# Summing the modulation columns with transposes and a free-axis reduction, in place of one-column matmuls

## The chip, the cores and the metric

The kernel runs on one core of one Trainium2 chip. The metric is the device time of one execution in microseconds, the median of a few runs. The engines of the core are named as in the profile: PE is TensorE (PEld its weight loads), DVE is VectorE, ACT is ScalarE, POOL is GpSimd and SP is SyncE, which here only issues DMAs. Each engine takes its instructions in the order in which they were written into its own queue and stops at the first one whose inputs are not there.

## The reference, cut to what matters

Two blocks follow each other on 256 tokens of width 2048. The first has two layers; each is steered by a modulation of two conditioning vectors, `c` (for the tokens) and `c_ctx` (for 256 context tokens):

```
def _layer(x, ctx, c, c_ctx, ...):
    shift, scale, gate = split(silu(c) @ w_mod + b_mod, 3)      # 2048 -> 3 * 2048
    hx = rmsnorm(x, norm_w) * (1 + scale) + shift
    a_h, a_b, a_c, a_z, q, k, v, r_z = split_in(hx @ w_in)
    mod_c = silu(c_ctx) @ w_mod + b_mod                         # layer 1: shift and scale alone
    hc = rmsnorm(ctx, norm_w) * (1 + mod_c[d:2*d]) + mod_c[:d]
    ...                                                         # retention and convolution branches
    x = x + gate * (concat(y_conv, y_ret) @ w_out)
    ctx = ctx + mod_c[2*d:] * (concat(yc_conv, yc_ret) @ w_out) # layer 0 alone
```

The second block (attention, a feed-forward part, a gated projection) uses no modulation.

## The kernel before, in words

All large products run on PE as split products: a weight tile of 256 rows by 512 columns is loaded in fp32 (tile `raw`, pool `wraw` with four buffers, issued by SP), split into a high part by ACT (`whi`, L277) and a low part by DVE (`wlo`, L278), and multiplied in three passes (L332). `Block.run` goes over the 16 k-tiles of a weight two at a time; two k-tiles are a unit, so a block of 512 columns has 8 units. PE's order is written by hand: it is the order of the calls in the program. The other engines' instructions are put in order by a scheduler that goes by priorities; the split has a raised one, as have the statistics of a norm (`hot()`).

Small work is woven between the units. `pump()` (L264) is called after every unit and lets each queue in `pumps` take a step. A queue is a `Side` object (L226): it holds generators, and a step runs one of them to its next `yield`. The queue `modq` holds `mod_bg` and steps at a rate: two steps in three units in layer 0 (`Side(1, 1, 2, 3)`, L898), one in three in layer 1 (L918). `drain()` (L251) runs what is left at once.

`mod_bg` (L422) computes the modulation on DVE, one block of 512 columns at a time. For each of eight pairs of k-tiles it loads 256 rows by 512 columns of `w_mod` (L429) and adds each row, times the partition's value of silu(c) or silu(c_ctx), to an accumulator [128, 512] (`macc0` for the first vector, `macc1` for the second, one buffer each): L435 for the first row block, L438 for the other 15. That is one step, and there are eight of them. The accumulator then still has to be summed over its 128 partitions, and the sums have to stand with features on partitions, 128 to a column. This is what L441 to L447 do: four matmuls for each vector with the accumulator as weights and a column of ones as the moving operand, and `mod_add` (L449, L450), which adds the bias.

The first call of `mod_bg`, queued before layer 0, has 12 column blocks with two vectors: the gates of layer 0 and the shift and scale of layer 1. What is not done at the end of layer 0 is drained there (L904). The second call has 4 column blocks with one vector, the gates of layer 1.

What surrounds the end of layer 0: the last block of `w_out` (L850), its result added to the streams `xr` and `cr_` (tags `a` and `b`) on DVE (L856), their squares on ACT (L871) and the sums of squares on DVE (L872, tiles `sqa`); then `modq.drain()`; then the modulation columns times the norm weight (L907); then `pli_proj` (L877), a product that depends on neither block and that stands there to occupy PE, with the norm's sums (L209), rsqrt on POOL (L195) and broadcast (L219, L220) between its pieces; then layer 1, whose operands (`make_hx`, L497) need the norm and all shift and scale columns of layer 1.

PSUM is split into five main tiles (`mm`) and three side tiles (`sd`, `side_ps`), the latter shared by retention, norms, transposes and the modulation sums.

Of the kernel before, what the change touches and what calls it, by code (L numbers as in the profile page):

```python
# [30 lines left out]

# columns of the constant tables
CA = {}
# [17 lines left out]

# rows of the packed feature vectors
VEC_ROWS = [
# [60 lines left out]
def kernel(ctx: ExitStack, tc: tile.TileContext, x, c, cx, c_ctx, norm_w, w_mod, b_mod,  # L114
# [31 lines left out]

    # ------------------------------------------------------------------ small tables
    ca = mk(consts, [P, NCA], "ca")
# [38 lines left out]

    # ------------------------------------------------------------------ helpers
    def hot():
# [14 lines left out]
    def tok_sums(accs):  # L204
        """per-token sums over the features of [128 feature, 256 token] tiles, tokens on partitions"""
        ps = side_ps()
        for a, acc in enumerate(accs):
            for t in range(2):
                nc.tensor.matmul(ps[:, 2 * a + t:2 * a + t + 1], lhsT=acc[:, t * P:(t + 1) * P],  # L209
                                 rhs=ones[:, 0:1], start=True, stop=True)  # L210
        return ps[:, :2 * len(accs)]

    def bcast_rows(r, n, tag):
        """[128 token, n] columns to a [128, n*128] tile with the value of each token on all partitions"""
        ps = side_ps()
        for t in range(n):
            dg = mk(sm, [P, P], "dg")
            with hot():
                nc.vector.tensor_scalar(out=dg, in0=ident, scalar1=r[:, t:t + 1], scalar2=None, op0=ALU.mult)  # L219
            nc.tensor.matmul(ps[:, t * P:(t + 1) * P], lhsT=ones, rhs=dg, start=True, stop=True)  # L220
        o = mk(sm, [P, n * P], tag, bufs=1)
        with hot():
            nc.scalar.copy(out=o, in_=ps[:, :n * P])
        return o

    class Side:  # L226
        """side work in steps, woven between the units of the products: at most `act` items under way,
        `rate` steps per unit, num units in den"""

# [27 lines left out]
    def pair(pool, n, tag):  # L257
        """room for the hi and lo parts of n columns"""
        b = mk(pool, [P, 2, n], tag, F32R)
        return b[:, 0, :], b[:, 1, :], b  # L260
# [20 lines left out]
    class Block:  # L281
        """columns cols = [(first, width)] of a weight against the moving operands mov(k) -> (hi, lo).
        fm: features on partitions, a [128, T] tile per 128 columns; tm: tokens on partitions, a
        [128, width] tile per column group and 128 tokens"""

        def __init__(self, w, cols, mov, T, mode, nk, dst=None):
            self.w, self.cols, self.mov, self.T, self.mode, self.nk = w, cols, mov, T, mode, nk
            self.done = 0
            self.dst = dst or self.room
            self.nt = [wd // P if mode == "fm" else T // P for _, wd in cols]  # L290
            # the hi and lo parts of 256 columns move as one operand; their products are added at the end
            self.wide = mode == "fm" and T == L
            self.ps = None
# [12 lines left out]
        def steps(self, kk, parts=None):  # L306
            """kk: consecutive k-tiles, at most 2; a step per tile of the result"""
            if self.ps is None:
# [43 lines left out]

    # ------------------------------------------------------------------ first block
    p1 = ExitStack()
# [25 lines left out]

    # silu of the two conditioning vectors: hi and lo parts as four columns, and plain
    load_vec(0)
# [9 lines left out]

    # x and the context, features on partitions; 1/rms of each token
    xr = [None] * KT
# [23 lines left out]

    # modulation: [layer][vector] columns, 16 each of shift, 1 + scale, gate
    modc = [[mk(consts, [P, 48], f"mod{l}{v}") for v in range(2)] for l in range(2)]  # L420

    def mod_bg(todo):  # L422
        """modulation on the vector engine: (layer, column blocks, vectors)"""
        for l, cols, nv in todo:
            for cb in cols:
                acc = [mk(t1, [P, 512], f"macc{v}") for v in range(nv)]
                for kc in range(0, KT, 2):
# [12 lines left out]
                    yield  # L440
                ps = side_ps()  # L441
                for v in range(nv):
                    for n in range(4):
                        nc.tensor.matmul(ps[:, 4 * v + n:4 * v + n + 1], lhsT=acc[v][:, n * P:(n + 1) * P],  # L444
                                         rhs=ones[:, 0:1], start=True, stop=True)
                for v in range(nv):
                    mod_add(l, v, cb * 4, 4, ps[:, 4 * v:4 * v + 4])  # L447

# [5 lines left out]
    def mod0_cols(j, weave):  # L454
        """shift and scale of layer 0 for the k-tiles 2j and 2j+1: the products"""
        pr = side_ps()
# [18 lines left out]
    def mod0_turn(j):  # L475
        """the same to columns, features on partitions"""
        ps = side_ps()
        for n in range(4):
            nc.tensor.matmul(ps[:, 2 * n:2 * n + 2], lhsT=rows[j][:, n * P:(n + 1) * P], rhs=C("comb", 4),  # L479
                             start=True, stop=True)  # L480
        v8 = ps[:, :8].rearrange("p (a n v) -> p a n v", a=2, v=2)
        for v in range(2):
            for a in range(2):
                mod_add(0, v, a * KT + 2 * j, 2, v8[:, a, :, v])
                if a:
                    m = modc[0][v][:, KT + 2 * j:KT + 2 * j + 2]
                    nc.vector.tensor_tensor(out=m, in0=m, in1=V["nw0"][:, 2 * j:2 * j + 2], op=ALU.mult)
# [3 lines left out]
    def put_split(dst, col, src):  # L491
        """hi and lo parts of src into dst at column col"""
        hi, lo = (d[:, col:col + src.shape[-1]] for d in dst[:2])
# [15 lines left out]
    def layer_tables(l):  # L509
        """log decays on all partitions, and their powers at each token"""  # L510
        lg = []
# [16 lines left out]
    def retention(l, h, qT, kT, v, streams, Y):  # L528
        """head h; qT, kT: [128, T]; v: [128, token tile, 128]"""
        lgf, lgb = (e[:, h:h + 1] for e in lgt["lg"])  # L530
        dec = lgt["dec"]
        # decay mask, keys on partitions
        dm = mk(at, [P, 4, P], "dm")
# [10 lines left out]
        nc.vector.tensor_copy(out=dm[:, 3, :], in_=dm[:, 0, :])  # L544
        # states of the context
        ps = side_ps()
# [81 lines left out]
    def layer(l):  # L628
# [21 lines left out]
        def rope(dst):  # L650
            """rows of x rotate by the token's position"""
            sw = mk(big, [P, 4, L], "big0")
# [6 lines left out]
        def qkv(g):  # L659
            nonlocal at  # L660
            if l == 0 and g == 0:
                # the k-tiles of the operand become ready as the modulation's columns do
                b = Block(wl, [(col("k", 0), 512), (col("q", 0), 256)], mov, T, "fm", KT)
# [209 lines left out]

    # p @ w_pli_proj does not depend on the blocks: it fills the tensor engine where a norm is awaited
    zd = dram.tile([L, D], F32, tag="zd", name="zd")
# [48 lines left out]

    # ------------------------------------------------------------------ second block
    p2 = ExitStack()
# [7 lines left out]
    def scaled_split(dst, src, col):  # L934
        """hi and lo parts of src * col (a factor per partition)"""
        hi, lo = dst[:2]
# [5 lines left out]

    # the norm at the end of the first block and the one before the mixer act after the product
    fl = mk(hp, [P, KT], "fl")
# [17 lines left out]
    def prologue():  # L962
# [18 lines left out]
        yield  # L981
        # bias of the dilated heads by distance, laid out for the band of a block of queries
        rel = mk(c2, [32, 8], "rel")
# [15 lines left out]
    def head_out(po, f, h):  # L999
        """rms norm of the two token tiles of a head, times f (a factor per token), to the operands"""  # L1000
        ss = mk(a2, [P, 2], "hss")
# [21 lines left out]
    def stick(h, qT, kT, n, vh):  # L1023
        # logits, keys on partitions: keys 0 against all queries, keys 1 against queries 1
        ps = side_ps()
# [32 lines left out]
    def dilated(h, qT, kT, n, vh):  # L1058
        # logits, queries on partitions: queries 1 against all keys, queries 0 against keys 0
        ps = side_ps()  # L1060
# [59 lines left out]
    def project(w, mov, korder, split_at):  # L1120
        """rows on partitions: F[t, c] is 256 columns of 128 tokens"""
        for cbs in ((0, 1), (2,), (3,)):
# [20 lines left out]
    def post_norm(gain, next_gain, first, also=None):  # L1143
        """residual plus the normed rows F, the next norm's operands, and its first block"""
        with hot():
# [34 lines left out]
    def x_stats(b):  # L1180
        """1/rms of the rows of x, behind the first units of b"""
        for k in range(KT):
# [108 lines left out]
```

## Time and profile before

| | |
|---|---|
| median of 3 runs | 2921.57 us (2920.47 to 2921.82) |
| span of the profiled execution | 2918.6 us |
| PE busy | 2885.2 us, 99% of the span |
| PE weight loads | 2387.2 us, 82% |
| DVE busy | 1829.0 us, 63% |
| ACT busy | 1292.7 us, 44% |
| DMA read | 509.88 MB |

The page gives the span of the profiled execution and no other time of it; the median of the runs lies 2.97 us above this span. Layer 0's part that is woven with `modq` lies between about 160 us and 1074 us, layer 1 from there to about 1660 us. In a timeline, a row gives the start, the duration, engine, line, operation, output and inputs, the shape and a count; an entry in brackets is idle time of the engine ahead of the row and what ended it. Matmuls overlap in the pipeline, so what one costs is the distance from start to start, and not its duration. The same holds, to a smaller degree, for DVE.

### The profile page before, as it was taken

To read this page: it belongs to the slowest core of one execution; us is meant where nothing else is said; L and a number is where in the kernel's file an instruction comes from. 1 tells how busy PE (TensorE), PEld (TensorE's weight loads), DVE (VectorE), ACT (ScalarE), POOL (GpSimd) and SP (SyncE) were. 2 spreads that over 40 slices of the span, in tenths; PEclk is the share of its full clock that TensorE was granted. 3 is DMA by queue.
4 is the path that set the end of the run, shared out by engine and by line. 5 is a ranking of instruction groups with operands and counts; after the bars stand their busy time and mean duration, and the time that the engine had idled before them with its cause. 6 is when DMAs were issued, how large, how long until landed. Compare 5 with 4: busy or idle time off the path is not lost.

```text
span 2918.6 us, 38376 instructions
## 1 busy us (share of the span) xinstructions
PE 2885.2 (99%) x14413; PEld 2387.2 (82%) x14413; DVE 1829.0 (63%) x2981; ACT 1292.7 (44%) x2048; POOL 82.3 (3%) x143
## 2 busy tenths in 40 slices
PE   7999999999999999999999999999999999999999
PEld 4678888888888878888888888887888888888878
DVE  7875765666667556663767776665765566544465
ACT  7633322242233233443545655554644454444354
POOL 0000000000000000000000010000000000000000
PEclk9999999999999999999999999999999999999999
DMA  9984445444556444654756665555555555555655
GB/s 306 299 242 141 127 152 159 145 138 133 159 162 199 159 133 144 207 178 143 222 178 222 201 196 173 166 169 176 163 186 187 188 186 185 186 187 188 202 172 167
DMA packets 299923, 527.11 MB, mean 181 GB/s; under 512 B 20016, under 2 KB 75800, under 8 KB 299480
## 3 DMA queue, kind: packets, MB, share of 16 engines
q1 hardware_dynamic: 296200, 513.23, 55.6%
q0 software_dynamic: 3392, 11.29, 1.3%
q8 instruction: 113, 1.85, 0.3%
q14 instruction: 74, 0.61, 0.1%
q10 hardware_dynamic: 144, 0.14, 0.0%
HBM read 509.88 MB, written 12.07 MB: 179 GB/s over the span
## 4 chain that ended last, share of the span: by engine, by line
PE 96%; DVE 1%; DMA 1%; ACT 0%; issue 0%; SPq 0%; POOL 0%; DVEq 0%; ACTq 0%; POOLq 0%
PE mm L332 89%; PE sd L466 2%; PE sd L444 1%; PE sd L581 1%; PE sd L568 1%; DMA raw<-in_w_mod_dram 1%; DVE wlo L278 1%; PE sd L332 0%; PE sd L575 0%; PE sd L559 0%; ACT whi L277 0%; PE sd L479 0%; POOL rq L195 0%; PE sd L410 0%; DMA kT<-in_x_dram 0%
## 5 line engine op out<-in xcount | busy, mean ns | idle before, releaser
L278 DVE TENSOR_TENSOR wlo<-raw,whi 128x1024 fp32r<-128x1024 f32 (+1 forms) x812 | 978.0, 1207 | 828.3 <-ACT whi L277 799.7
L277 ACT CAST whi<-raw 128x1024 fp32r<-128x1024 f32 (+1 forms) x812 | 841.0, 1037 | 1400.6 <-PE mm L332 1183.4
L332 PE MATMUL mm<-a,whi 128*128 128x512 f32 x3392 | 1115.2, 398 | 0.9 <-DVE a L505 0.5
L332 PE MATMUL mm<-a,wlo 128*128 128x512 f32 (+1 forms) x2208 | 755.5, 342 | 0.0
L332 PEld LDWEIGHTS mm<-a,whi 128*128 128x128 f32 x3392 | 634.8, 188 | 146.8 <-ACT a L504 0.8
L332 PE MATMUL mm<-h,whi 128*128 128x512 f32 x1920 | 682.9, 400 | 0.5 <-DVE h L938 0.5
L332 PE MATMUL mm<-h,wlo 128*128 128x256 f32 x1920 | 539.1, 281 | 0.0
L332 PEld LDWEIGHTS mm<-a,wlo 128*128 128x128 f32 x2208 | 415.3, 188 | 54.7
L332 PEld LDWEIGHTS mm<-h,whi 128*128 128x128 f32 x1920 | 360.8, 188 | 89.4 <-DVE h L938 0.7
L332 PEld LDWEIGHTS mm<-h,wlo 128*128 128x128 f32 x1920 | 362.8, 189 | 0.0
L438 DVE SCALAR_TENSOR_TENSOR macc<-raw,s,macc 128x512 f32<-128x512 f32 x420 | 291.9, 746 | 87.7 <-DMA raw<-in_w_mod_dram 86.8
L332 PE MATMUL mm<-whi,f 128*128 128x512 f32 x704 | 221.5, 395 | 0.0
L332 PE MATMUL mm<-whi,h 128*128 128x512 f32 (+1 forms) x576 | 172.0, 373 | 0.0
L332 PE MATMUL mm<-whi,a 128*128 128x512 f32 x512 | 161.9, 395 | 0.0
L332 PEld LDWEIGHTS mm<-whi,f 128*128 128x128 f32 x704 | 132.4, 188 | 31.9
L332 PE MATMUL mm<-wlo,f 128*128 128x512 f32 x352 | 139.2, 396 | 0.0
L332 PEld LDWEIGHTS mm<-whi,h 128*128 128x128 f32 x576 | 104.6, 189 | 16.6
L332 PEld LDWEIGHTS mm<-whi,a 128*128 128x128 f32 x512 | 96.1, 188 | 23.1
L332 PE MATMUL mm<-wlo,h 128*128 128x512 f32 (+1 forms) x288 | 105.7, 367 | 0.0
L332 PE MATMUL mm<-wlo,a 128*128 128x512 f32 x256 | 101.5, 396 | 0.0
L332 PE MATMUL mm<-whi,o 128*128 128x512 f32 x256 | 81.7, 397 | 0.0
L332 PEld LDWEIGHTS mm<-wlo,f 128*128 128x128 f32 x352 | 66.2, 188 | 15.9
(309 smaller groups left out, 2199.8 us busy)
## 6 DMA issues: line engine op xcount, KB each, us to landing
raw<-in_w_in_dram SPq DMA_DIRECT2D x344, 512.0 KB, 3.9
raw<-in_w_gate_up_dram SPq DMA_DIRECT2D x176, 512.0 KB, 3.4
raw<-in_w_mod_dram SPq DMA_DIRECT2D x128, 512.0 KB, 4.3
raw<-in_w_out_dram SPq DMA_DIRECT2D x96, 512.0 KB, 4.2
raw<-in_w_down_dram SPq DMA_DIRECT2D x88, 512.0 KB, 3.9
raw<-in_w_mod_dram SPq DMA_DIRECT2D x128, 256.0 KB, 5.6
raw<-in_w_pli_gate_dram SPq DMA_DIRECT2D x24, 512.0 KB, 4.3
raw<-in_w_in_dram SPq DMA_DIRECT2D x16, 256.0 KB, 5.3
```

Source lines behind the costliest of these rows:

```text
L277: nc.scalar.copy(out=hi, in_=raw)
L278: nc.vector.tensor_tensor(out=lo, in0=raw, in1=hi, op=ALU.subtract)
L332: nc.tensor.matmul(o[b], lhsT=l_, rhs=r_, start=d0 + a == 0 and b == 0, stop=d0 + a == self.nk - 1 and b == len(tri) - 1)
L438: nc.vector.scalar_tensor_tensor(out=acc[v], in0=raw[:, a, :], scalar=sc, in1=acc[v], op0=ALU.mult, op1=ALU.add)
L444: nc.tensor.matmul(ps[:, 4 * v + n:4 * v + n + 1], lhsT=acc[v][:, n * P:(n + 1) * P], rhs=ones[:, 0:1], start=True, stop=True)
L466: nc.tensor.matmul(pr[:4, :], lhsT=s4[:, kc + a, :], rhs=w[:, a, :], start=(kc + a == 0 and b == 0), stop=(kc + a == KT - 1 and b == 1))
L568: nc.tensor.matmul(ps[:, t * L:(t + 1) * L], lhsT=kT[:, q0 + t * P:q0 + (t + 1) * P], rhs=qT[:, q0:q0 + L], start=True, stop=True)
L581: nc.tensor.matmul(po[:, t * P:(t + 1) * P], lhsT=sc[:, jt * L + t * P:jt * L + (t + 1) * P], rhs=v[:, 2 * s + jt, :], start=(jt == 0), st ...
```

## The change

For each column block and each vector, `mod_bg` now takes a side tile of its own, transposes the four [128, 128] parts of the accumulator into it on PE (the identity is the other operand), sums each of the four transposed parts along the free axis with one `tensor_reduce` on DVE into a [128, 4] tile `mcol`, and calls `mod_add` with it. After each vector there is a `yield`. Comments and docstrings are gone as well; with one line more in `mod_bg`, what stands behind it has moved by one line (L872 is now L873, for example).

```
                     yield
-                ps = side_ps()
                 for v in range(nv):
+                    ps = side_ps()
                     for n in range(4):
-                        nc.tensor.matmul(ps[:, 4 * v + n:4 * v + n + 1], lhsT=acc[v][:, n * P:(n + 1) * P],
-                                         rhs=ones[:, 0:1], start=True, stop=True)
-                for v in range(nv):
-                    mod_add(l, v, cb * 4, 4, ps[:, 4 * v:4 * v + 4])
+                        nc.tensor.transpose(ps[:, n * P:(n + 1) * P], acc[v][:, n * P:(n + 1) * P], ident)
+                    col = mk(sm, [P, 4], "mcol")
+                    nc.vector.tensor_reduce(out=col, in_=ps.rearrange("p (n t) -> p n t", n=4), axis=AX.X, op=ALU.add)
+                    mod_add(l, v, cb * 4, 4, col)
+                    yield
```

The order of the instructions changes most at the end of layer 0. On PE, before, the last product of `w_out` (tiles `a14`, `a15`) is followed at once by `pli_proj` (`big0`):

```order
L332 MATMUL mm_1426_8081<-a14_1258_7046,whi_1450_8305 128x512 x2
L332 MATMUL mm_1426_8081<-a14_1258_7046,wlo_1451_8306 128x512
L332 MATMUL mm_1426_8081<-a15_1259_7051,whi_1450_8305 128x512 x2
L332 MATMUL mm_1426_8081<-a15_1259_7051,wlo_1451_8306 128x512
L332 MATMUL sd_1460_8367<-whi_1463_8371,big0_1380_7761 128x512
L332 MATMUL sd_1460_8367<-wlo_1464_8372,big0_1380_7761 128x512
```

Before, the last modulation sums stand 97 rows ahead of this place. On PE at the same place, now:

```order
L332 MATMUL mm_1429_7992<-a14_1261_6975,whi_1458_8233 128x512 x2
L332 MATMUL mm_1429_7992<-a14_1261_6975,wlo_1459_8234 128x512
L332 MATMUL mm_1429_7992<-a15_1262_6980,whi_1458_8233 128x512 x2
L332 MATMUL mm_1429_7992<-a15_1262_6980,wlo_1459_8234 128x512
L444 MATMUL sd_1478_8343<-ca_1_83,macc0_1460_8261 128x128 x4
L444 MATMUL sd_1480_8351<-ca_1_83,macc1_1461_8262 128x128 x4
L444 MATMUL sd_1492_8409<-ca_1_83,macc0_1482_8359 128x128 x4
L444 MATMUL sd_1494_8417<-ca_1_83,macc1_1483_8360 128x128 x4
L332 MATMUL sd_1496_8427<-whi_1499_8431,big0_1381_7670 128x512
```

The transposes of the last two column blocks (accumulators 1460 and 1461, then 1482 and 1483) have come between the last product of `w_out` and the first of `pli_proj`.

On DVE, at the end of layer 0's sums of squares, before:

```order
L856 SCALAR_TENSOR_TENSOR b15_1369_7720<-mm_1426_8081,mod01_15_129,b15_1369_7720 128x256
L872 TENSOR_TENSOR sqa1_3_86<-sqa1_3_86,tmp_1455_8346 128x256
L872 TENSOR_TENSOR sqa0_2_85<-sqa0_2_85,tmp_1456_8350 128x256
L872 TENSOR_TENSOR sqa1_3_86<-sqa1_3_86,tmp_1457_8354 128x256
L278 TENSOR_TENSOR wlo_1482_8434<-raw_1480_8431,whi_1481_8433 128x1024
```

Before, DVE goes on from there to the low parts for `pli_proj` and layer 1. On DVE at the same place, now, from the last sum of squares on:

```order
L873 TENSOR_TENSOR sqa0_2_85<-sqa0_2_85,tmp_1469_8294 128x256
L873 TENSOR_TENSOR sqa1_3_86<-sqa1_3_86,tmp_1470_8298 128x256
L438 SCALAR_TENSOR_TENSOR macc1_1461_8262<-raw_1473_8313,s2_12_122,macc1_1461_8262 128x512
L438 SCALAR_TENSOR_TENSOR macc0_1460_8261<-raw_1474_8319,s2_12_122,macc0_1460_8261 128x512
L438 SCALAR_TENSOR_TENSOR macc1_1461_8262<-raw_1474_8319,s2_12_122,macc1_1461_8262 128x512
```

The rest of the 11th column block, 16 instructions of L438, now stands behind the sums of squares. On DVE, where that block ends and the 12th begins, now:

```order
L438 SCALAR_TENSOR_TENSOR macc0_1460_8261<-raw_1477_8337,s2_12_122,macc0_1460_8261 128x512
L438 SCALAR_TENSOR_TENSOR macc1_1461_8262<-raw_1477_8337,s2_12_122,macc1_1461_8262 128x512 x2
L446 TENSOR_REDUCE mcol_1479_8348<-sd_1478_8343 128x4
L435 TENSOR_SCALAR macc0_1482_8359<-raw_1484_8361,s2_12_122 128x512
L451 SCALAR_TENSOR_TENSOR mod10_16_130<-mcol_1479_8348,vecs_4_87 128x4
L446 TENSOR_REDUCE mcol_1481_8356<-sd_1480_8351 128x4
L435 TENSOR_SCALAR macc1_1483_8360<-raw_1484_8361,s2_12_122 128x512
L451 SCALAR_TENSOR_TENSOR mod11_17_131<-mcol_1481_8356,vecs_4_87 128x4
L438 SCALAR_TENSOR_TENSOR macc0_1482_8359<-raw_1484_8361,s2_12_122,macc0_1482_8359 128x512
```

Behind the last row shown come 29 more instructions of L438, with two of L278 for `pli_proj` among them (`wlo_1500` and `wlo_1507`), and all of the 12th column block's products now stand behind the end of `w_out`.

## Rows read from the trace of the kernel before

**Rows 1.** The page: engines' busy time, the chain's lines, the group of L438

```profile
PE 2885.2 (99%) x14413; PEld 2387.2 (82%) x14413; DVE 1829.0 (63%) x2981; ACT 1292.7 (44%) x2048; POOL 82.3 (3%) x143
...
PE mm L332 89%; PE sd L466 2%; PE sd L444 1%; PE sd L581 1%; PE sd L568 1%; DMA raw<-in_w_mod_dram 1%; DVE wlo L278 1%; PE sd L332 0%; PE sd L575 0%; PE sd L559 0%; ACT whi L277 0%; PE sd L479 0%; POOL rq L195 0%; PE sd L410 0%; DMA kT<-in_x_dram 0%
...
L438 DVE SCALAR_TENSOR_TENSOR macc<-raw,s,macc 128x512 f32<-128x512 f32 x420 | 291.9, 746 | 87.7 <-DMA raw<-in_w_mod_dram 86.8
```

**Rows 2.** Line L444: duration ns min/median/max, first and last start us

```profile
L444 PE MATMUL sd<-ca,macc x224: 164/250/250, 227.3 to 1489.9; 128*128 128x1 f32 x112
```

**Rows 3.** PE's timeline about the first column block's sums

```profile
227.11 0.40 PE L332 MATMUL mm<-whi,a 128*128 128x512 f32 x1
227.34 1.84 PE L444 MATMUL sd<-ca,macc 128*128 128x1 f32 x16
229.04 0.49 PE L332 MATMUL mm<-whi,a 128*128 128x512 f32 x1
229.37 0.39 PE L332 MATMUL mm<-wlo,a 128*128 128x512 f32 x1
```

**Rows 4.** PE's timeline about eight transposes in a stream of products

```profile
2821.94 0.60 PE L1233 MATMUL sd<-ca,a 128*128 128x128 f32 x4
2822.37 0.60 PE L1169 MATMUL sd<-ca,b 128*128 128x128 f32 x4
2822.73 0.48 PE L332 MATMUL mm<-whi,h 128*128 128x512 f32 x1
2823.04 0.39 PE L332 MATMUL mm<-wlo,h 128*128 128x512 f32 x1
```

**Rows 5.** Line L608, transposes of retention: duration ns min/median/max

```profile
L608 PE MATMUL sd<-ca,o x48: 270/271/308, 281.4 to 1498.8; 128*128 128x128 f32 x48
```

**Rows 6.** Line L1069, reductions on DVE: duration ns min/median/max

```profile
L1069 DVE TENSOR_REDUCE dmx<-e x16: 267/350/417, 1790.8 to 1953.7; 128x1 f32<-128x256 f32 x8, 128x1 f32<-128x128 f32 x8
```

**Rows 7.** DVE's timeline behind the first column block

```profile
229.22 0.23 DVE L450 SCALAR_TENSOR_TENSOR mod<-sd,vecs 128x4 f32<-128x4 f32 x2 [0.41 <-PE sd L444]
229.37 0.48 DVE L435 TENSOR_SCALAR macc<-raw,s 128x512 f32<-128x512 f32 x1
229.76 1.22 DVE L278 TENSOR_TENSOR wlo<-raw,whi 128x1024 fp32r<-128x1024 f32 x1
230.89 4.72 DVE L438 SCALAR_TENSOR_TENSOR macc<-raw,s,macc 128x512 f32<-128x512 f32 x7
```

**Rows 8.** DVE's timeline: the last modulation columns of layer 0's weaving

```profile
1040.34 0.23 DVE L450 SCALAR_TENSOR_TENSOR mod<-sd,vecs 128x4 f32<-128x4 f32 x2 [5.22 <-PE sd L444]
```

**Rows 9.** PE's timeline: `pli_proj` begins behind `w_out` of layer 0

```profile
1073.98 0.40 PE L332 MATMUL sd<-whi,big 128*128 128x512 f32 x1
```

**Rows 10.** DVE's timeline at the same place: residuals and sums of squares

```profile
1070.55 0.48 DVE L856 SCALAR_TENSOR_TENSOR a<-mm,mod,a 128x256 f32<-128x256 f32 x1
...
1074.63 0.47 DVE L856 SCALAR_TENSOR_TENSOR b<-mm,mod,b 128x256 f32<-128x256 f32 x1
1075.02 1.09 DVE L872 TENSOR_TENSOR sqa<-sqa,tmp 128x256 f32<-128x256 f32 x3
1076.03 1.22 DVE L278 TENSOR_TENSOR wlo<-raw,whi 128x1024 fp32r<-128x1024 f32 x1
1077.16 0.75 DVE L872 TENSOR_TENSOR sqa<-sqa,tmp 128x256 f32<-128x256 f32 x2
```

**Rows 11.** Windows: length, busy us (count) by engine, granted clock, DMA share, GB/s

```profile
1040.00:1060.00 20.00, 20.00 (x88) 16.14 (x88) 5.27 (x8) 3.16 (x3) 0.00 (x0) 1.00 0.24 79
```

**Rows 12.** PE's timeline: its longest wait behind the start, near the end

```profile
2810.13 0.40 PE L332 MATMUL mm<-whi,f 128*128 128x512 f32 x1
2814.39 3.79 PE L1163 MATMUL sd<-dg,b 128*128 128x128 f32 x16 [3.86 <-DVE dg L1153]
```

**Rows 13.** Windows behind that wait, columns as in rows 11

```profile
2814.00:2816.00 2.00, 1.61 (x7) 1.61 (x8) 0.88 (x3) 1.96 (x5) 0.55 (x2) 0.50 0.56 175
2816.00:2818.00 2.00, 2.00 (x12) 2.00 (x11) 1.56 (x5) 1.98 (x6) 0.00 (x0) 0.50 0.96 301
2818.00:2820.00 2.00, 2.00 (x9) 1.80 (x8) 2.00 (x6) 2.00 (x6) 0.00 (x0) 0.60 0.78 328
2820.00:2822.00 2.00, 2.00 (x11) 1.58 (x10) 1.27 (x3) 1.47 (x4) 0.00 (x0) 1.00 0.00 0
```

**Rows 14.** Line L429, loads of modulation weights: from issue to landing

```profile
DMA to landing us min/median/max: 3.5/4.3/5.5
```

## The prediction, made before the run

> **What bounds the kernel now.** I read the page first. PE is busy for 99% of the span, and the chain that ended last runs along PE's products; the modulation sums of L444 are 1% of that chain by themselves [rows 1]. So whatever PE spends on L444 is paid in full, and whatever makes PE wait is paid too. DVE is busy for 63% and mostly waits for others; more work on it is free where PE does not wait for it. Then I read PE's timeline about L444 to price the work removed, transposes elsewhere in the program to price the work added, and last the order of the changed kernel, to see where each engine meets the new instructions. The order settles this case.
>
> **PE: the sums removed.** L444 has 112 matmuls, 28 groups of four (24 groups in pairs, 4 alone), and 224 records, so each fp32 matmul is two passes [rows 2]. In the first column block two groups start at 227.34; the product behind them starts at 229.04 and the next at 229.37, while the normal distance is 0.23 us (227.11 to 227.34). Eight matmuls therefore cost 229.37 - 227.34 - 0.23 = 1.80 us, or 0.225 us each [rows 3]. All 112 cost 25.2 us.
>
> **PE: the transposes added.** They are 112 too, with the same shapes as those of L1233 and L1169, eight of which stand in a stream of products: 2823.04 - 2821.94 - 0.23 = 0.87 us, or 0.109 us each [rows 4]. All 112 cost 12.2 us. The balance on PE is 12.2 - 25.2 = **-13.0 us**, in full on the path.
>
> A rule of the Trainium skill speaks against this. The page "TensorE: Matmul & The Clock Gate", section "Part 4: PE-mode transpose", gives about 275 ns for a transpose in a kernel and says that the full clock does not engage for them. The trace agrees with that as a duration (271 ns), but its starts are 0.109 us apart. What the kernel would do if the duration were the price is a rival below.
>
> **DVE: the reduction added.** 28 reductions of 512 elements to 4 columns. The trace has none of this size; its reductions take 267 ns for 128 elements and 417 ns for 256 [rows 6], so 150 ns for 128 more: 417 + 300 = 717 ns. Bounds: 417 ns below, and twice 717 above in case PSUM or four output columns cost more. At 0.72 us they add 20 us to DVE, hidden in the weaving, where DVE has over 14 of 20 us free in a stretch such as 1040 to 1060 [rows 11]. L450 reads `mcol` now and stays at 0.15 us or so.
>
> **The step count.** This is where the change costs. `mod_bg` yields 8 times for a column block before, and 10 times now with two vectors. After `modq` joins the pumps, layer 0 runs 19 blocks (15 in `qkv`, convolution and gates, 4 of `w_out`) of 8 units: 152 pumps, and at two steps in three 101 steps. Before, 12 column blocks need 96 steps and end in time: the last columns come at 1040.34 [rows 8], 33.6 us before `pli_proj` begins on PE at 1073.98 [rows 9]. Now they need 120. The 101 steps cover ten blocks; the 11th and 12th fall to the drain. The order shows it: PE has their 16 transposes between the last product of `w_out` and `pli_proj`, the work that should occupy it there. PE goes by its written order, so it stops at the first of the four groups until DVE has made the sums. The eleventh block's products were partly scheduled ahead; 16 of L438 stand behind the sums of squares, and of the 12th block everything does, because its accumulators have one buffer each and wait for the transposes.
>
> The wait, counted from the moment T0 when the last `w_out` product is through:
>
> - A. DVE must first do the residuals and squares of the last four tiles. Before, it does 8 of L856 and 8 of L872 between 1070.55 and 1077.91, T0 + 3.9, with one L278 of 1.1 us in it [rows 10]. Without that L278, but with one L438 between them and a later start (the accumulator's load comes just before), I take T0 + 3.8; bounds 2.0 to 5.
> - B. 16 of L438. Seven in a row take 4.72 us with 0.746 for one, so (4.72 - 0.75)/6 = 0.663 us from start to start [rows 1, 7]: 10.6 us; at most 11.9 at 0.746.
> - C. Two reductions, two L435 and two L451, at start-to-start distances of 0.65, 0.40 and 0.1 [rows 6, 7]: 2.3 us; PE's eight transposes run beside it.
> - D. 30 of L438 and two L278 at 1.14 (229.76 to 230.89) [rows 7]: 19.9 + 2.3 = 22.2 us; up to 24.7.
> - E. The last four transposes after an idle spell, at half speed, and a wake-up: 1.2 us.
>
> The sum is 40.1 us; 16 transposes are already in the balance above (1.7 us), so the **wait is 38.4 us**. With the bounds of A, B and D, and reductions from 0.42 to 1.4 us, it lies between 36 and 45. The loads keep up: four buffers, 4.3 us from issue to landing [rows 14], and 4 x 0.663 = 2.65 us of DVE work per load.
>
> **PE's clock.** After a wait of 3.86 us the granted clock read 0.50 for the next windows, i.e. 1.2 of 2.4 GHz, and was back near 2819.2, after some 5 us of work from 2814.39 on [rows 12, 13]. Half of that is lost: 2.5 us. PE waits far longer here, so `pli_proj` begins at half clock: **+2.6 us**, between 0 and 5.
>
> Behind the drain I expect no second wait: the `pli_proj` weights are split by then or follow within 1 or 2 us, and the norm's chain stands where it stood. In layer 1, 4 x 9 = 36 steps meet 160/3 = 53: nothing is left over.
>
> **Sum.** -13.0 + 38.4 + 2.6 = +28.0 us. The profiled span would be 2946.6 us; the median stands 2.97 us above the span, so the forecast for the runs is 2921.6 + 28.0 = **2949.6 us**, 1.0% slower. Its own range is 2921.6 - 13.0 + 36 + 0 = 2944.6 to 2921.6 - 13.0 + 45 + 5 = 2958.6; DVE running ahead of my count in A and B would take off another 3.
>
> **Rivals.**
>
> 1. The tail is hidden, and the kernel is faster. DVE is idle for three quarters of the last `w_out` block [rows 11]: from 1040 to 1074 that is 25 us, room for 38 of the 62 products (two blocks of 31 with their L435). If products ran ahead there, PE would find the sums ready: 2921.6 - 13.0 = 2908.6 us. It decides at 13.0/0.663, about 19 of L438 or less behind T0, the clock's loss left out. Against it: 46 stand behind the residuals in DVE's order, and the 12th block cannot start before the 11th is transposed, which PE does only after `w_out`.
>
> 2. The drain is bound by loads. Nine loads are issued after T0. If each had to be issued and land alone, 4.3 + 0.4 us instead of 2.65, they would add 9 x 2.05 = 18 us: 2968 us. For it: DVE already waits 86.8 us for these loads [rows 1]. Against it: there SP's queue mixes them with weight loads that wait for buffers; in the drain it holds little else.
>
> 3. A transpose costs its duration, 0.271 us [rows 5]: 112 x 0.271 = 30.4 us against 25.2, so +5.2 in place of -13.0: 2968 us. Rows 4 speak against it.
>
> 4. The reductions or the extra side tile make PE wait in the weaving: each column block takes two of the three side tiles a unit apart where it took one. At 0.3 to 0.5 us for each of 28 groups that is 8 to 14 us on top, 2958 to 2964 us. Against it: DVE has slack and the low parts are two units ahead.
>
> **How the numbers follow.** The forecast has 0.74, rival 1 0.05, rival 2 0.08, rival 3 0.03, rival 4 0.07; 0.03 is left for a small net effect, in which the wait is mostly hidden. The range runs from 2941 us (the forecast's low end less the 3 us) to 2964 us, which takes in rival 4. A change of 0.2%, 5.8 us, is about what a measurement of this kernel can tell from none. Faster than that: rival 1, 0.05. Same: 0.03. Slower: 0.92.
>
> **What would show it.** In the changed kernel's profile PE's largest wait must be at L444, ended by DVE's L438, in two pieces near 1065 us: about 15 us and about 24 us. L444 must have 112 records instead of 224 with starts about 0.11 us apart. The reductions of L446 should be near 0.72 us. The window behind the wait must show the granted clock near 0.5. If PE is busy through the end of layer 0, the step argument is wrong; if the wait is there but over 50 us, the loads bound it; if L444's starts are 0.27 apart, rival 3 holds.

## The result, and the profile after

The changed kernel takes 2950.06 us (median of 4 runs, 2948.75 to 2956.69) against 2921.70 us for the kernel before (4 runs): a ratio of 1.0100, 95% interval 1.0087 to 1.0113. It is 28.4 us slower; 28.0 us were forecast, and 2949.6 us. The profiled execution has a span of 2947.7 us, 29.1 us more than before. One thing limits what differences below 10 us can tell: beside three of the later runs the kernel before was run 15 times, and four of these executions took 2912.4 to 2913.1 us, the other eleven 2920.0 to 2923.7; no profile shows why.

In the changed kernel the sums have one line more, so lines from L451 on stand one further than before (the residual L856 is L857, `mod_add` L450 is L451).

The page: busy time and share of each engine, then the busy tenths of PE and its granted clock in 40 slices, and the group of L438.

```profile
span 2947.7 us, 38156 instructions
PE 2877.2 (98%) x14301; PEld 2377.1 (81%) x14301; DVE 1850.2 (63%) x3009; ACT 1292.1 (44%) x2048; POOL 84.4 (3%) x143
PE   7999999999999959999999999999999999999999
PEclk9999999999999979999999999999999999999999
L438 DVE SCALAR_TENSOR_TENSOR macc<-raw,s,macc 128x512 f32<-128x512 f32 x420 | 297.7, 748 | 138.1 <-DMA raw<-in_w_mod_dram 135.2
```

PE does 8.0 us less than in [rows 1] and still ends 29 us later. The slice with the 5 is the end of layer 0, about 1032 to 1105 us. Nothing of this kind stood in the kernel before.

The new instructions, PE's sums and DVE's reduction: duration of one (least, median, most) in ns, first and last start.

```profile
L444 PE MATMUL sd<-ca,macc x112: 270/272/476, 227.1 to 1538.3; 128*128 128x128 f32 x112
L446 DVE TENSOR_REDUCE mcol<-sd x28: 681/692/694, 227.7 to 1538.6; 128x4 f32<-128x512 f32 x28
```

There are 112 records of L444 in place of the 224 of [rows 2]. Four transposes in PE's timeline (start, duration, and, in brackets where there is any, the idle time before it and what ended it):

```profile
227.08 0.60 PE L444 MATMUL sd<-ca,macc 128*128 128x128 f32 x4
227.44 0.48 PE L332 MATMUL mm<-whi,a 128*128 128x512 f32 x1
227.76 0.40 PE L332 MATMUL mm<-wlo,a 128*128 128x512 f32 x1
```

They take 227.76 - 227.08 - 0.23 = 0.45 us of PE's time, 0.11 us each, though each record lasts 0.27 us. The matmuls with ones took 0.225 us each [rows 3].

PE's waits from 1060 to 1560 us (what waits, for what: us in total, times, longest):

```profile
PE sd L444 <- DVE macc L438: 35.5, 3, 23.1
PE mm L332 <- DVE b L338: 1.4, 1, 1.4
PE mm L332 <- ACT a L505: 1.0, 1, 1.0
PE sd L220 <- DVE dg L219: 0.8, 1, 0.8
```

One wait makes the result. PE's timeline shows where it is, between the last `w_out` product and the first of `pli_proj`:

```profile
1060.63 0.40 PE L332 MATMUL mm<-a,wlo 128*128 128x512 f32 x1
1073.00 1.12 PE L444 MATMUL sd<-ca,macc 128*128 128x128 f32 x4 [11.97 <-DVE macc L438]
1074.55 1.09 PE L444 MATMUL sd<-ca,macc 128*128 128x128 f32 x4 [0.42 <-DVE macc L438]
1098.78 1.94 PE L444 MATMUL sd<-ca,macc 128*128 128x128 f32 x8 [23.15 <-DVE macc L438]
1100.37 0.78 PE L332 MATMUL sd<-whi,big 128*128 128x512 f32 x1
```

The same stretch in DVE's timeline:

```profile
1061.92 1.76 DVE L873 TENSOR_TENSOR sqa<-sqa,tmp 128x256 f32<-128x256 f32 x5
1063.59 10.81 DVE L438 SCALAR_TENSOR_TENSOR macc<-raw,s,macc 128x512 f32<-128x512 f32 x16
1074.31 0.68 DVE L446 TENSOR_REDUCE mcol<-sd 128x4 f32<-128x512 f32 x1
...
1076.74 16.65 DVE L438 SCALAR_TENSOR_TENSOR macc<-raw,s,macc 128x512 f32<-128x512 f32 x25
1093.62 1.23 DVE L278 TENSOR_TENSOR wlo<-raw,whi 128x1024 fp32r<-128x1024 f32 x1 [0.23 <-ACT whi L277]
...
1097.88 1.41 DVE L438 SCALAR_TENSOR_TENSOR macc<-raw,s,macc 128x512 f32<-128x512 f32 x2
```

DVE works almost without a gap: 16 products of the 11th column block, its reductions, 30 products of the 12th. PE has eight transposes to do in the 38 us before the last eight. From 1020 to 1040 us DVE had been busy for 5.5 of 20 us only: PE had the transposes of the 10th block further on in its order, at 1043.1 and 1049.2, and the 11th block, which needs the same accumulators, began behind them. From 1040 to 1060 DVE was busy for 15.7 of 20 us, and 14 of the 11th block's 30 products of L438 ran there. In that place the kernel before shows 5.3 of 20 us [rows 11]; what DVE had free in the changed kernel was before 1040.

Windows over the wait and behind it (length, then busy time and count of PE, PEld, DVE, ACT and POOL; the granted clock is the third number from the end, in front of the DMA share and GB/s):

```profile
1062.00:1074.00 12.00, 1.00 (x4) 0.72 (x4) 11.96 (x22) 0.76 (x2) 0.00 (x0) 0.60 0.53 149
1076.00:1098.00 22.00, 0.00 (x0) 0.00 (x0) 21.77 (x34) 2.09 (x2) 0.00 (x0) 0.50 0.64 192
1100.00:1102.00 2.00, 2.00 (x8) 1.71 (x7) 2.00 (x3) 0.00 (x0) 0.00 (x0) 0.50 0.90 324
1102.00:1104.00 2.00, 2.00 (x9) 1.61 (x9) 0.61 (x6) 0.59 (x1) 0.30 (x1) 0.99 1.01 339
```

PE begins `pli_proj` at half clock (1.2 of 2.4 GHz) and has the full clock again from 1102 on.

Set beside the kernel before at the same places of PE's program, the difference of the two profiled executions builds up like this:

| place on PE | before, us | after, us | difference |
|---|---|---|---|
| end of the last `w_out` product, layer 0 | 1074.1 | 1061.0 | -13.1 |
| first product of `pli_proj` | 1074.0 | 1100.4 | +26.4 |
| first product of layer 1 | 1088.7 | 1115.2 | +26.5 |
| last transposes of L548 in layer 1 | 1463.6 | 1492.4 | +28.8 |
| end of the span | 2918.6 | 2947.7 | +29.1 |

The gain of 13.1 us is fully there when layer 0 ends. The wait takes 39.5 us. Layer 1 loses 2.3 us more.

### The profile page after: what moved, and what is told of

Its sections match the earlier page's. It is cut to its first block, busy times and chain, and to the rows that moved or that the text cites. A ratio compares the mean times of both kernels' runs of the same rounds, so it can differ in the third digit from the quotient of the medians.

```text
span 2947.7 us, 38156 instructions
## 1 busy us (share of the span) xinstructions
PE 2877.2 (98%) x14301; PEld 2377.1 (81%) x14301; DVE 1850.2 (63%) x3009; ACT 1292.1 (44%) x2048; POOL 84.4 (3%) x143
## 3 DMA queue, kind: packets, MB, share of 16 engines
q8 instruction: 112, 1.84, 0.3%
## 5 line engine op out<-in xcount | busy, mean ns | idle before, releaser
L278 DVE TENSOR_TENSOR wlo<-raw,whi 128x1024 fp32r<-128x1024 f32 (+1 forms) x812 | 977.8, 1208 | 797.7 <-ACT whi L277 776.5
L332 PE MATMUL mm<-a,whi 128*128 128x512 f32 x3392 | 1116.5, 399 | 3.4 <-DVE b L338 1.4
L438 DVE SCALAR_TENSOR_TENSOR macc<-raw,s,macc 128x512 f32<-128x512 f32 x420 | 297.7, 748 | 138.1 <-DMA raw<-in_w_mod_dram 135.2
```

The source lines that it names most:

```text
L278: nc.vector.tensor_tensor(out=lo, in0=raw, in1=hi, op=ALU.subtract)
L332: nc.tensor.matmul(o[b], lhsT=l_, rhs=r_, start=d0 + a == 0 and b == 0, stop=d0 + a == self.nk - 1 and b == len(tri) - 1)
L438: nc.vector.scalar_tensor_tensor(out=acc[v], in0=raw[:, a, :], scalar=sc, in1=acc[v], op0=ALU.mult, op1=ALU.add)
```

## Experiments

The theory is the prediction's: PE gains 13 us from the new form of the sums, and the `yield` behind each vector, 24 of them, pushes two column blocks into the drain. The rivals are that the new instructions themselves cost something in the weaving or by their duration, and that the drain has another price than the count of DVE's products. Each kernel ran on one chip with the kernel before, whose median there was between 2920.44 and 2921.51 us; the ratios are to that.

### The new sums without the yield, the yield without the new sums, and a faster queue

The first leaves the yield out of the changed kernel.

```diff
                     mod_add(l, v, cb * 4, 4, col)
-                    yield
```

> The changed kernel without the yield behind each vector: the transposes and the reductions stay, a column block is 8 steps again, and all 12 blocks are done before the end of layer 0. My theory (the steps made the wait, PE's own work fell by 13.0 us): 2921.7 - 13.0 = 2908.7 us, between 2905 and 2912, and no wait at L444. Rival (the transposes and reductions themselves hold PE up): it stays near 2950 us. Rival (a transpose costs its whole duration of 0.27 us): 2927 us.

Measured: 2911.20 us, ratio 0.9965 (0.9953 to 0.9978). The second keeps the matmuls with ones and gives the kernel before the yields.

```diff
                 for v in range(nv):
                     mod_add(l, v, cb * 4, 4, ps[:, 4 * v:4 * v + 4])
+                    yield
```

> The kernel before with a yield behind each vector, and nothing else: the one-column matmuls stay, a column block is 10 steps. 43 products stand behind the residuals at the end of layer 0. My theory (the steps make the wait, whatever the sums are made with): wait 2.7 + 43 x 0.663 + two L435, two splits and eight one-column sums, about 36 us, and 1 to 3 us behind it: 2921.7 + 38 = 2960 us, between 2953 and 2965. Rival (the wait comes from the transposes, the reduction or the second side tile): 2922 us.

Measured: 2959.3 us, ratio 1.0130 (1.0110 to 1.0150), with four executions between 2953.0 and 2964.7. Its waits of PE from 1060 to 1130 us have the changed kernel's line:

```profile
PE sd L444 <- DVE macc L438: 33.9, 2, 22.6
```

That the time met the forecast of 2960 us is luck in part: from the last `w_out` product to `pli_proj` it took 41.1 us where about 36 were expected, but layer 0 ended 4.1 us earlier than in the kernel before, 3.6 us of which are the 16 sums of the last two blocks (16 x 0.225), which lie in the drain.

The third keeps both and lets the queue step on five pumps in six instead of two in three, so that 152 pumps give 126 steps where 120 are needed.

```diff
-    modq = Side(1, 1, 2, 3)
+    modq = Side(1, 1, 5, 6)
```

> The changed kernel, yields included, with the modulation queue stepping five times in six units in layer 0 in place of two in three: 152 x 5/6 = 126 steps against the 121 needed, so nothing is drained. My theory: 2908.7 us as without the yields, between 2905 and 2913; DVE has somewhat more to do per unit. Rival (two side tiles a unit apart, or reductions on DVE, stall PE in the weaving): clearly above 2912 us, up to 2922.

Measured: 2911.68 us, ratio 0.9967 (0.9954 to 0.9980), and PE has no wait at L444.

These three settle the main question. The yields cost 2950.1 - 2911.2 = 38.9 us with the new sums and 2959.3 - 2921.5 = 37.8 us with the old ones, so the loss has nothing to do with transposes or reductions. Giving the queue enough steps takes it all away with the yields still in place, so it is the step count and not the yield as such. The new form of the sums alone is a gain of 10 us (by the interval of the first 6.4 to 13.7).

### Half of the yields

One yield per block of two vectors: 9 steps a block, 108 in all, against 101.

```diff
                     mod_add(l, v, cb * 4, 4, col)
-                    yield
+                    if v < nv - 1:
+                        yield
```

> The changed kernel with a yield between the two vectors alone: 9 steps for a column block with two vectors, 108 in all against 101, so only a part of the 12th block is drained. 16 products and the last eight transposes stand behind the residuals. My theory (the wait grows with the products left): 2.7 + 16 x 0.663 + 1.5 = 14.8 us, 0.9 of it counted in the balance: 2921.7 - 13.0 + 13.9 + 1 = 2923.6 us, between 2919 and 2928. Rival (a drain costs as much whatever its length): 2950 us.

Measured: 2936.07 us, ratio 1.0052 (1.0037 to 1.0067), 12 us over what was expected. PE's waits in layer 1 and the drain, 1075 to 1490 us (lines here are two further than before):

```profile
PE sd L444 <- DVE macc L438: 14.9, 2, 13.5
PE mm L332 <- DVE b L338: 2.9, 2, 1.8
PE mm L332 <- DVE big L338: 1.4, 1, 1.4
```

The wait at the drain is near the theory: from the last `w_out` product (the next would start at 1061.9) to `pli_proj` at 1078.8 it is 16.9 us where 14.8 were expected; two splits, which the sum had left out, stand among the 16 products. The larger part of the miss is elsewhere: from the first product of layer 1 to its last L548 this kernel takes 383.0 us, the kernel before 374.9. That opened a second question, which the last group of runs answers.

### The drain behind `pli_proj`

If PE waits in the drain, `pli_proj` can fill that wait, as it needs nothing of the sums. The drain and the loop on `modc` move behind it.

```diff
     layer(0)
-    modq.drain()
-    for v in range(2):
-        m = modc[1][v][:, KT:2 * KT]
-        nc.vector.tensor_tensor(out=m, in0=m, in1=V["nw1"], op=ALU.mult)
     for _ in range(3):
...
     for _ in fill:
         pass
+    modq.drain()
+    for v in range(2):
+        m = modc[1][v][:, KT:2 * KT]
+        nc.vector.tensor_tensor(out=m, in0=m, in1=V["nw1"], op=ALU.mult)
```

> The changed kernel with the drain, and the product of the modulation columns with the norm weight, moved behind the whole of the projection that fills PE at the norm. Nothing else moves. My theory (PE waits only because the last 16 transposes stand ahead of 15 us of work that needs nothing from them; the work on DVE stays as long): that work hides about 11 to 14 us of the 39 us, splits for it on DVE take back some 3: 2950 - 10 = 2940 us, between 2935 and 2944. Rival (the projection is bound by the same DVE queue and waits with the sums): 2950 us.

Measured: 2953.97 us, ratio 1.0120 (1.0103 to 1.0137): no gain at all, 4 us above the changed kernel. PE's timeline:

```profile
1083.84 1.94 PE L444 MATMUL sd<-ca,macc 128*128 128x128 f32 x8 [8.62 <-DVE macc L438]
1107.88 1.94 PE L444 MATMUL sd<-ca,macc 128*128 128x128 f32 x8 [22.09 <-DVE macc L438]
1116.46 1.44 PE L332 MATMUL mm<-a,whi 128*128 128x512 f32 x2 [6.65 <-ACT a L505]
```

And DVE's:

```profile
1066.29 1.41 DVE L438 SCALAR_TENSOR_TENSOR macc<-raw,s,macc 128x512 f32<-128x512 f32 x2
...
1070.36 14.00 DVE L438 SCALAR_TENSOR_TENSOR macc<-raw,s,macc 128x512 f32<-128x512 f32 x21
...
1087.10 16.65 DVE L438 SCALAR_TENSOR_TENSOR macc<-raw,s,macc 128x512 f32<-128x512 f32 x25
```

`pli_proj` did run inside the wait, right behind `w_out`, and the time came back behind it. Two things were left out of the forecast. DVE, not PE, sets the length of this stretch, and its products now stand behind the splits and norm factors that `pli_proj` brings with it: 54 of them lie behind 1066 us (in the changed kernel 46 behind 1063.6), and the last transposes start at 1107.88 instead of 1098.78. And the operands of layer 1 need these columns. In the changed kernel they are formed while `pli_proj` runs; here PE has nothing left and waits 6.65 us for them. Layer 1 begins at 1116.5 us, 1.3 us later than in the changed kernel, and behind that wait its first 8 us run at a mean granted clock of 0.63, which loses another 3.0 us.

### The prices of the new instructions

Both start from the kernel without the yield. In the first every transpose is done twice, in the second every reduction.

```diff
-                    for n in range(4):
+                    for n in (0, 1, 2, 3, 0, 1, 2, 3):
                         nc.tensor.transpose(ps[:, n * P:(n + 1) * P], acc[v][:, n * P:(n + 1) * P], ident)
```

> Without the yields, and every transpose of the sums done twice into the same place: 112 more of them, nothing else. It measures a transpose in this stream of products. By starts that are 0.109 us apart: 12.2 us above the kernel without yields, 2921 us if that is at 2908.7. By the duration of 0.271 us: 30 us above it, 2939 us.

Measured: 2924.51 us, ratio 1.0019 (1.0009 to 1.0029), 13.3 us above the kernel without the yield, so 0.119 us for each of the 112 added. By the intervals this difference is certain to some 5 us, so the price lies between about 0.08 and 0.16. Its first block on PE:

```profile
227.20 1.91 PE L444 MATMUL sd<-ca,macc 128*128 128x128 f32 x16
228.87 0.48 PE L332 MATMUL mm<-whi,a 128*128 128x512 f32 x1
229.18 0.40 PE L332 MATMUL mm<-wlo,a 128*128 128x512 f32 x1
```

Sixteen take 229.18 - 227.20 - 0.23 = 1.75 us, 0.109 us each.

```diff
                     nc.vector.tensor_reduce(out=col, in_=ps.rearrange("p (n t) -> p n t", n=4), axis=AX.X, op=ALU.add)
+                    nc.vector.tensor_reduce(out=col, in_=ps.rearrange("p (n t) -> p n t", n=4), axis=AX.X, op=ALU.add)
```

> Without the yields, and every reduction done twice: 28 x 0.65 = 18 us more on DVE. My theory (in the weaving DVE has room, and nothing waits for these columns): as without the yields, within 2 us. Rival (DVE's time counts): up to 18 us more.

Measured: 2911.16 us, ratio 0.9971 (0.9958 to 0.9984), the time without the second reduction (2911.20). Another 19 us on DVE cost nothing that shows (the two intervals leave room for some 5 us), and the rival that the reduction holds PE up in the weaving falls.

### What layer 1 loses: the phase of a counter

`Side.step` counts its calls in `c` and makes a step when `c * num // den` grows. In layer 1 `modq` steps on every third pump, and which third depends on where `c` stands when layer 1 begins. Other numbers of steps in layer 0 and in the drain leave it elsewhere. The first runs had suggested this: all with a remainder of 0 took about 375 us for the stretch of layer 1, all with 2 took longer (a remainder of 1 was never run). Three runs set `c` by hand; the first is the kernel with half of the yields.

```diff
-    modq.num, modq.den = 1, 3
+    modq.num, modq.den, modq.c = 1, 3, 0
```

> The kernel with one yield per block (e4), whose step counter is set back to 0 between the drain and layer 1. That counter decides on which third pump the modulation makes its step in layer 1. At the start of layer 1 it stands at 156 in the kernel before, in e1 and in e3 (156 mod 3 = 0), at 164 in e4 and at 176 in the changed kernel and in e2 (both 2 mod 3). From the first product of layer 1 to its last L548 transposes the first three took 374.9, 374.4 and 375.4 us, e4 383.0, the changed kernel 377.2, e2 380.3. Theory: the 12 us that e4 was over its forecast are mostly this phase, which puts the modulation's steps beside other results of DVE on which TensorE then waits (L338, 2.9 and 1.4 us). Then layer 1 takes about 375 us again and the median falls by some 8 us from 2936.1 to 2928 (2925 to 2931), with the wait of 14.9 us at the drain unchanged. Rival: the excess hangs on the drain itself (layer 1 starts with its loads and operands in another state), not on the counter: then the median stays at 2936 (2934 to 2938).

Measured: 2925.88 us, ratio 1.0017 (1.0008 to 1.0027), 10.2 us less, with PE's wait for L438 at the drain still 14.8 us. The second is the changed kernel with the same edit.

> The changed kernel with the step counter set back to 0 between the drain and layer 1 (it stands at 176, 2 mod 3, there without that). Theory of the phase: layer 1 loses the 2.3 us that it has over the kernel before (377.2 against 374.9 us), the median falls from 2950.1 to 2947.8 (2946 to 2950). Rival, that the small waits of layer 1 come from the yield that stands behind each vector there (9 steps a block in place of 8) or from the drain: no change, 2950 (2949 to 2951).

Measured: 2949.45 us, ratio 1.0096 (1.0081 to 1.0111). The stretch in layer 1 shrank by the expected 2.3 us, but the medians differ by 0.6 us, so the time doesn't decide between the two theories. The profiles show where the 2.3 us went: against the changed kernel's, this execution ended layer 0 1.2 us later and lost 2.3 us more behind layer 1, in code that is the same in both. The third is the kernel without the yield, with `c` set to 2.

> The changed kernel without its yield (e1, median 2911.2), with the step counter set to 2 between the drain and layer 1, where e1 has 156 (0 mod 3). In layer 1 its steps are those of e4. Theory of the phase: it gets e4's waits in layer 1, 8 us more, 2919 (2915 to 2921), with no wait at the drain. Rival, that e4's excess hangs on its drain: as e1, 2911 (2909 to 2913).

Measured: 2920.64 us, ratio 0.9999 (0.9990 to 1.0009): 9.4 us of the 10.3 us gain are gone by a counter alone, without any drain. All the kernels, with the stretch from the first product of layer 1 to its last L548, each from one profiled execution:

| kernel | `c` at layer 1, remainder by 3 | stretch, us |
|---|---|---|
| before | 156, 0 | 374.9 |
| no yield | 156, 0 | 374.4 |
| faster queue | 156, 0 | 375.4 |
| double transposes | 156, 0 | 375.7 |
| double reduction | 156, 0 | 374.2 |
| half of the yields, `c` set | 0 | 373.5 |
| changed kernel, `c` set | 0 | 374.9 |
| changed kernel | 176, 2 | 377.2 |
| drain behind `pli_proj` | 173, 2 | 377.9 |
| old sums with yields | 176, 2 | 380.3 |
| half of the yields | 164, 2 | 383.0 |
| no yield, `c` set to 2 | 2 | 384.6 |

One row says nothing of the phase: of the 377.9 us with the drain behind `pli_proj`, 3.0 are the clock lost behind its wait of 6.65 us. The others with a remainder of 2 lie 2.3 to 10.2 us above their partners with 0, so the remainder alone does not set the price.

How a phase costs time is to be seen in the kernel without the yield and `c` at 2. PE's waits from 1060 to 1560 us:

```profile
PE mm L332 <- DVE b L338: 2.9, 2, 1.8
...
PE mm L332 <- DVE big L338: 0.9, 1, 0.9
...
PE mm L332 <- DVE wlo L278: 0.7, 1, 0.7
```

DVE's timeline at the longest of them:

```profile
1245.83 2.35 DVE L278 TENSOR_TENSOR wlo<-raw,whi 128x1024 fp32r<-128x1024 f32 x2
1250.75 1.54 DVE L438 SCALAR_TENSOR_TENSOR macc<-raw,s,macc 128x512 f32<-128x512 f32 x2 [2.57 <-DMA raw<-in_w_mod_dram]
1252.20 0.75 DVE L338 TENSOR_TENSOR b<-mm,b 128x256 f32<-128x256 f32 x2
```

And PE's:

```profile
1250.55 0.28 PE L332 MATMUL mm<-a,wlo 128*128 128x256 f32 x1
1252.67 0.50 PE L332 MATMUL mm<-a,whi 128*128 128x512 f32 x1 [1.84 <-DVE b L338]
```

DVE stands 2.57 us at the modulation's product, whose load has not landed. Behind it in DVE's order is L338, which empties PE's result tiles, and PE waits 1.84 us for that. In the kernel without this edit (`c` at 156, remainder 0) the modulation's products nearest to that L338 come two splits ahead of it and meet data that is there, and L338 itself waits for nothing:

```profile
1240.75 1.54 DVE L438 SCALAR_TENSOR_TENSOR macc<-raw,s,macc 128x512 f32<-128x512 f32 x2
...
1245.09 1.08 DVE L338 TENSOR_TENSOR b<-mm,b 128x256 f32<-128x256 f32 x3
```

The waits that the profile lists grow by 4.6 us (7.4 against 2.8), and PE's idle time over the whole stretch by 5.0 us (6.4 against 1.4). A part of the rest is the clock. Behind the wait it was granted at 0.57 for four microseconds, where the kernel without the edit has 1.00:

```profile
1254.00:1258.00 4.00, 3.92 (x15) 3.12 (x15) 4.00 (x9) 2.06 (x4) 0.00 (x0) 0.57 0.83 243
1258.00:1262.00 4.00, 4.00 (x24) 3.52 (x24) 3.46 (x7) 3.16 (x9) 0.00 (x0) 1.00 0.76 257
```

That is 0.43 x 4 = 1.7 us. A second such place is the begin of layer 1, first with `c` at 2, then without the edit:

```profile
1080.00:1088.00 8.00, 6.35 (x18) 4.16 (x18) 8.00 (x18) 6.63 (x13) 1.62 (x3) 0.79 0.56 183
1079.00:1087.00 8.00, 6.56 (x28) 4.73 (x27) 8.00 (x18) 6.28 (x12) 1.62 (x3) 1.00 0.55 174
```

Here 0.21 x 8 = 1.7 us are lost; the kernel with half of the yields and a remainder of 2 has the same 0.79 there, and with `c` set to 0 it has 1.00. Idle time and clock together give 8.4 of the 10.2 us by which the stretch is longer than without the edit; the remaining 1.8 us stay unexplained.

## Why the prediction was right, step by step

- **PE: the balance of -13.0.** In the changed kernel it is there: -13.1 us when layer 0 ends, where the prices give 96 x 0.225 - 80 x 0.109 = 12.9 us by then. That they agree so closely is luck: the same layer 0 ends 12.0 us early in the changed kernel with `c` set. 112 records and starts 0.11 us apart, as written. In time the sums alone were worth 10.3, 9.8 and 9.3 us in the three kernels that isolate them (no yield, faster queue, double reduction). The interval of the first reaches to 13.7, but three times about 3 us less suggests that something comes back. Their profiled executions begin the second block 10.4, 10.8 and 10.4 us ahead of the kernel before and end 5.8, 8.2 and 8.0 ahead, so 2.4 to 4.6 us go in code that the change leaves alone; the changed kernel loses 0.5 us there, with `c` set 2.8. Whether that belongs to the kernels or to the one profiled execution of the kernel before stays open. The higher price of a transpose that the doubling gives (0.119 for 0.109, 1.1 us in all) is within its error.
- **The price of a transpose.** The rival of 0.271 us each, 2968 us, is excluded by the doubled transposes, 0.119 us each (0.16 at most). The 275 ns that the Trainium skill gives for one ("TensorE: Matmul & The Clock Gate", "Part 4: PE-mode transpose") agree with the duration of a record here, 272 ns, and not with what one costs in a stream; the measurement decides.
- **The reduction.** 717 ns were estimated, 692 ns came. It costs nothing, as its doubling shows.
- **The step count.** Right, and shown from four sides: no yield, old sums with yields, more steps, half of the yields.
- **The wait.** A was T0 + 2.7 in place of 3.8 (DVE's squares end at 1063.6, `w_out` at 1060.9); B 10.7 for 10.6; C 2.4 for 2.3; D 22.0 for 22.2 (1076.74 to 1098.78); E 1.6 for 1.2 (1098.78 to 1100.37). The sum is 39.5 us from T0 to `pli_proj` against 40.1. PE's two waits are 12.0 and 23.2 us where about 15 and 24 were named. The low bound of the range had allowed for DVE running ahead in A by even more. That the loads keep up held: DVE is busy for 21.77 of 22 us.
- **The clock, +2.6.** Over-sized. `pli_proj` ran at half clock from 1100.37 to 1102 only, which loses 0.8 us. From the first transposes at 1098.78 the clock took 3.2 us to come back, against the 5 us read from [rows 12, 13] (by the 0.60 of the third window the clock was back at 2819.6, not at 2819.2, so 5.2), and half of the 3.2 were in E. PE also waits 0.7 us less for L219 inside `pli_proj` (0.8 in place of 1.5), so the stretch came out only 0.1 us longer.
- **"Behind the drain I expect no second wait."** This step failed, by 2.3 us in the table of places, or 3.7 by the prices, which give the 12 cheaper sums of that stretch 1.4 us (12 x 0.116; the kernel without the yield, with the same sums, takes only 0.5 us less there than the kernel before). The prediction counted the steps of layer 1 (36 of 53), which was right, and did not ask on which pumps they fall. That they fall elsewhere can cost 8 to 10 us, as two of the other kernels show. Here it was small, and the two errors of size, the clock and A, stood on the other side. That the total came within 0.5 us is luck: it was closer than its terms.
- **The rivals.** A hidden tail did not come, and the reason given against it held: the 12th block waits for the 11th. Loads did not bind the drain.

The kernel without the yield is faster than both: 2911.2 us, 0.35% below the kernel before.

## What to carry to other kernels

A step in a cooperative generator is a unit of a budget: before adding a yield, count the pumps that are left and the steps that are needed, and see which engine pays when the rest is drained at once. Filling a wait with other work of the waiting engine helps only if that engine sets the length of the stretch, so first ask which engine is without a gap in it. And in an engine that works in order, side work that waits for a DMA holds up everything behind it; where side steps are spread by a counter, its phase is part of the schedule, and a run with another phase tells how much of a small difference is only that.

## What was not expected of the hardware

PE's clock was back 3.2 us after work resumed behind a wait of 23 us, sooner than after the wait of 3.86 us in the kernel before (about 5 us, [rows 12, 13]). On the other side a wait of only 1.84 us, with one of 0.71 us some 4 us ahead of it, was followed by four microseconds at a granted clock of 0.57. And at the begin of layer 1 two waits of 0.85 and 0.64 us were followed by a clock of 0.50 for some three microseconds in the kernel without the yield and `c` at 2, while nearly the same two, 0.80 and 0.64 us, left it at 1.00 without that edit.
